# First feed-forward of a decoder layer: later activation sums, last differences used last, first half's residual by accumulating transfers, four squares later

## The chip, the cores and the metric

The kernel runs on one core of a Trainium2 chip. Its five engines work side by side, each through its own queue in order: TensorE (PE, matrix products), VectorE (DVE), ScalarE (ACT), GpSimd (POOL) and SyncE (SP, which here only starts transfers). An engine waits for another, or for a transfer, on semaphores. The metric is the device time of one execution in microseconds (us), lower is better; three runs of the kernel before took 2606.85, 2609.25 and 2610.62 us, so its median is 2609.25 us.

## The reference

One decoder layer on 1024 tokens of width 1024: a first SwiGLU feed-forward, a mixer (attention beside a state-space part), a cross-attention to a memory, and a second feed-forward. Each has a norm ahead and behind, and a residual. Only the first feed-forward and its residual matter here:

```python
def rmsnorm(x, g):
    return x * rsqrt(mean(x * x) + EPS) * g

def swiglu(h, w_gu, w_down):          # w_gu 1024 x 5632, w_down 2816 x 1024
    g, u = split(h @ w_gu, 2)
    return (silu(g) * u) @ w_down

h = x
f = swiglu(rmsnorm(h, ffn1_pre_g), ffn1_w_gu, ffn1_w_down)
h = h + 0.5 * rmsnorm(f, ffn1_post_g)
m = hybrid_mixer(rmsnorm(h, mix_pre_g), ...)      # goes on from h
```

## The kernel before

**Layout.** Activations lie transposed, features on the 128 partitions and tokens along the free axis. The 1024 tokens are two halves of 512 (`hh` 0 and 1), so one tile is 128x512. The 1024 model features are eight such tiles (`d` 0 to 7), the 2816 hidden features are 22 (`f` 0 to 21). A product in nearly full precision is made of three passes on TensorE: every operand is split into a high and a low part (`split`: ScalarE casts the high part, VectorE subtracts it from the whole for the low part), and the passes are high x high, low x high, high x low. A block of weights against four tiles of activations is therefore 12 matmuls of 128x128 by 128x512.

**Up-phase (`up_phase`).** For `f` 0 to 2 gate and up products are made plainly. From `f` = 3 (`first_seven`) on, `seven(f)` makes gate and up of one `f` for both token halves as a 2x2 product of blocks by seven products instead of eight. In order: `product(a,B22)`, `product(b,B21)`, `product(c,S[1])`, `product(m6,S[4])`, `product(a,B12)`, `product(c,S[5])`, `product(b,B11)`. The last three go on into banks `a`, `c` and `b`, which hold an earlier product. Bank `c` is the one to watch: `S[1]` is made in it, VectorE then reads it (`e = d + c`, line 823, where `d` is a difference that GpSimd makes of two copies, line 818), and only after this may `S[5]` be added to it. VectorE also reads `a` after B12 (line 833) and `b` after B11 (line 843), and the last step of an `f` is a multiplication on GpSimd (line 844).

The weight blocks of one `f` come from `pieces(f)`: seven sums and differences of quarters of the weights (GpSimd, line 757, tile `wc`), each then split into `whi`/`wlo`/`blk`. The fifth of them is a plain quarter (G0), the one that B12 takes, and is split from the loaded weights without a sum. The activations of B12 are tiles 0 to 3 of half 1: their low parts are the `xl` tiles numbered 28 to 31 below, made of differences (line 730) late in the run-up to `f` = 3.

**What sets the order.** Most side work is put into a list `later` with a due time on a model clock (`self.clock`) that advances with the matmuls written so far; when it is due it is written into the program there (`kp` keeps the place). Such work is: `act_sums`, which loads four stored activation tiles of two `f` back (line 609), makes five sums of them on VectorE (line 616) and stores these (line 621) for the down-phase; it runs for `f` 0 and 1 at `seven(4)` and for `f` 2 and 3 at `seven(5)`. `prepare_all`, which loads, splits and stores 62 half weight tiles for the mixer, one each 3.9 us of model time from 148 us on. What is written with `urgent` goes ahead of the queue of the scheduler.

**Down-phase (`down1`, `down7`).** Again seven products per pair of blocks, `m` = 0 to 6; weights `hl`, `wlo`, `whi`, `dx` are formed on VectorE (`cb`, line 1031) and split. As outputs become complete, `finish(m,i)` starts the norm behind: squares are summed (`squares`, `sumsq`: ScalarE squares, VectorE adds, line 363), `post` makes the factor rows, and per tile `apply(d)` multiplies (line 401), adds the residual that `resid` had loaded by a GpSimd transfer into `XL` (line 405), stores the new residual `h` by a GpSimd transfer (line 410), and casts the high part of the next input on ScalarE (`xh`, line 412). `low(d)` makes its low part (line 417) and `presum(d)` its square sums. Half 0 is finished while the products of `m` = 4 to 6 run, half 1 behind `m` = 6. Half 1's squares 0 to 3 are made during `m` = 6, its squares 4 to 7 as the last outputs come.

Of the kernel before, what the change touches and what calls it, by code (L numbers as in the profile page):

```python
# [14 lines left out]
ALU = mybir.AluOpType  # L15
# [32 lines left out]
class Kern:  # L48
# [189 lines left out]
    def prepare_all(self, sp):  # L238
        names = [("ssd", i) for i in [*range(6), *range(12, 26)]] + [("qkv", i) for i in range(QKV)]
        pairs = [  # L240
            ((self.fp, "acc0", None), (self.fp, "acc1", None)), ((self.fp, "rpost", None), (self.tp, "dg", None)),
            ((sp, "bh", None), (sp, "bl", None)),
        ]
        raw = [(sp, "braw", 2), (sp, "braw", 2), (self.xp, "xl0", KT + 1), (self.xp, "xl1", KT + 1)]
        n = 2 * len(names)
        self.prepare(names, raw, pairs, [148000 + 3900 * i for i in range(n)])

# [131 lines left out]

    def post(self, hh, gname, r2, gnext=None, out=None, step=None, spread=True, pins=(23000, 28000), accs=None, at=None, tail=None, hold=False):  # L380


        nc = self.nc
        t1, t2 = 2500, 6000
        if accs is None:
            accs = self.new_accs()
            for d in range(KT):
                self.sumsq(accs, d, self.F[hh][d])
# [9 lines left out]
        def apply(d):  # L398
# [4 lines left out]
                )  # L403
            )
            self.kp(nc.vector.tensor_tensor(out=F, in0=F, in1=self.XL[hh][d], op=ALU.add))  # L405
# [24 lines left out]

        def rest(d):
            low(d)
            presum(d)
# [16 lines left out]
        for d in range(KT):  # L450
            t = t3 + step * d
            q.append((t, lambda d=d: apply(d)))
            if out is None:
                q.append((t + min(step, 2600) + 300, lambda d=d: rest(d)))
        if out is None:
            t += min(step, 2600)
            c2 = self.t(self.rp, [P, 4], F32, f"cpre{hh}", bufs=2)
# [98 lines left out]
    def up_phase(self, sp, sp2, wgu, gpre, act_d, bank, load, plain, sizes, rw=None, begin=None):  # L556
# [40 lines left out]
        def act_sums(j, t0):  # L597

            x = {}
            names = ("a11", "a21", "a12", "a22")  # L600
            late = 14000 if begin else 9000

# [22 lines left out]
            for i, (n, out, a, b, op) in enumerate((  # L625
# [120 lines left out]
        def pieces(f):  # L746
# [3 lines left out]
            G0, G1, U0, U1 = G[:, 0:4], G[:, 4:8], U[:, 0:4], U[:, 4:8]  # L750
            for a, b, op in (
                (G0, G1, ALU.add), (U1, None, None), (G0, U1, ALU.add), (U0, G0, ALU.subtract), (G0, None, None),
                (G1, U1, ALU.subtract), (U0, U1, ALU.add),
            ):
                if b is not None:
                    t = self.t(sp if begin else sp2, [P, 4, P], F32, "wc", bufs=NWC)
                    inst = nc.gpsimd.tensor_tensor(out=t, in0=a, in1=b, op=op)  # L757
                    if begin and f == first_seven and a is G0 and b is G1:
                        self.tc.keep_in_program_order(inst)
# [44 lines left out]
        def seven(f):  # L804


            t5, d = (self.t(self.tp, [P, H], F32, f"sq{i}") for i in range(2))
            if later_sums and (f in (4, 5) if begin else f > 6 and f % 2):
                act_sums(later_sums.pop(0), self.clock)
# [19 lines left out]
            t1 = ft()  # L829
            with self.urgent():  # L830
                scaled(t1, a, 1)
            with self.urgent():
                nc.vector.tensor_tensor(out=e, in0=e, in1=a, op=ALU.add)
            product(c, S[5], True)
# [7 lines left out]
            with self.urgent():  # L842
                nc.vector.tensor_tensor(out=e, in0=e, in1=b, op=ALU.subtract)  # L843
            nc.gpsimd.tensor_tensor(out=t1, in0=t1, in1=e, op=ALU.mult)  # L844
            if f < 4:
# [106 lines left out]
    def down1(self, sp, wdn, act_d, xs_d, gpost, gnext):  # L952
# [7 lines left out]
        def squares(hh, d, tag):  # L960
            if d == 0:
                accs[:] = self.new_accs(tag)
            self.sumsq(accs, d, self.F[hh][d])

# [1431 lines left out]
```

## Time and profile before

| what | before |
|---|---|
| runs | 2606.85, 2609.25, 2610.62 us |
| profiled execution | span 2606.7 us from first to last instruction; no time outside the span is given for it |
| TensorE (PE) | 2578.2 us busy, 99% of the span, 12850 matmuls |
| VectorE (DVE) | 1993.9 us, 76% |
| ScalarE (ACT) | 1289.7 us, 49% |
| GpSimd (POOL) | 577.9 us, 22% |
| mean TensorE clock that was granted | 0.999 |

The profile is one execution, recorded by the hardware. A row of a timeline reads: start, duration (both in us), engine, source line, operation, output<-inputs by the program's names without buffer numbers, shapes, count; in square brackets how long the engine sat idle ahead of it and what released it. Several like instructions in a row are joined, with their count at the end. A PE row of 0.39 us is one matmul in a pipeline: its start and the next one's start matter, not its duration. In the windows view each stretch of time shows busy time and count of each engine, the granted clock (PEclk), the DMA share and the bytes moved.

Times of day in the span: `seven(3)` begins at about 79 us, `seven(4)` at about 102 us, the down-phase at about 449 us, half 0's norm is applied from 614 to 646 us, and the last down product ends at about 667 us.

### The profile page before, as it was taken

The numbers are of one execution on the slowest core, as the hardware profiler recorded it, in microseconds if no ns is written. First come the engines' busy times: TensorE is split into PE (matmuls) and PEld (weight loads), VectorE is DVE, ScalarE is ACT, GpSimd is POOL, SyncE is SP. The second block draws the span as 40 slices with busy tenths as digits, with TensorE's granted clock in tenths as the row PEclk, the third lists the DMA queues.
The fourth block names the chain that finished last, engine by engine and source line by source line (L and its number), as shares of the span: only waits on it lengthen the run. The fifth ranks groups of instructions, "written<-read, shape, count | busy, mean of one in ns | idle before, by whom it ended". The sixth has DMA issues, their size and how long they took to land.

```text
span 2606.7 us, 36814 instructions
## 1 busy us (share of the span) xinstructions
PE 2578.2 (99%) x12850; PEld 2148.5 (82%) x12850; DVE 1993.9 (76%) x3044; ACT 1289.7 (49%) x2300; POOL 577.9 (22%) x669
## 2 busy tenths in 40 slices
PE   9999999999999999999999999999999999999999
PEld 7788888888777778888888898888878888888887
DVE  7978987779689884777777777876656888777767
ACT  7434444555356663555555554445554433334543
POOL 2655554001000001111111110101011655551000
PEclk9999999999999999999999999999999999999999
DMA  6468887655656516555555556547558453326554
GB/s 241 158 210 298 300 287 272 209 188 169 224 195 204 182 69 213 162 149 152 141 152 131 169 161 215 206 153 250 196 185 299 146 183 104 109 85 236 184 174 154
DMA packets 216042, 489.82 MB, mean 188 GB/s; under 512 B 26544, under 2 KB 35120, under 8 KB 215856
## 3 DMA queue, kind: packets, MB, share of 16 engines
q1 hardware_dynamic: 169232, 381.02, 44.6%
q0 software_dynamic: 22720, 62.93, 8.1%
q10 hardware_dynamic: 23904, 43.53, 4.5%
q8 instruction: 101, 1.65, 0.3%
q14 instruction: 85, 0.70, 0.1%
HBM read 327.46 MB, written 138.94 MB: 179 GB/s over the span
## 4 chain that ended last, share of the span: by engine, by line
PE 77%; issue 13%; DVE 5%; ACT 1%; DMA 1%; POOL 0%; DVEq 0%; ACTq 0%; POOLq 0%
PE mm L139 38%; PE dn L139 34%; PE z L139 2%; PE tr L142 2%; PE ms L139 1%; PE ms L142 1%; DVE nb L1770 1%; DVE wlo L263 0%; DVE acc L363 0%; DVE hl L263 0%; DVE atl L263 0%; DVE F L1053 0%; DVE xl L263 0%; DVE F L405 0%; DVE xl L417 0%
## 5 line engine op out<-in xcount | busy, mean ns | idle before, releaser
L139 PE MATMUL mm<-xh,whi 128*128 128x512 f32 x1320 | 520.3, 403 | 2.5 <-ACT xh L268 1.1
L139 PE MATMUL mm<-xh,wlo 128*128 128x512 f32 x1272 | 488.7, 391 | 0.0
L139 PE MATMUL mm<-xl,whi 128*128 128x512 f32 (+1 forms) x1252 | 486.9, 389 | 1.8 <-DVE xl L263 1.4
L139 PEld LDWEIGHTS mm<-xh,whi 128*128 128x128 f32 x1320 | 248.2, 188 | 44.6 <-issue 3.8
L139 PEld LDWEIGHTS mm<-xh,wlo 128*128 128x128 f32 x1272 | 238.8, 188 | 52.1 <-DVE wlo L263 0.4
L139 PEld LDWEIGHTS mm<-xl,whi 128*128 128x128 f32 x1252 | 236.1, 189 | 35.9 <-DVE xl L263 2.3
L1770 DVE TENSOR_TENSOR_SCAN nb<-nb,begin 128x128 f32<-128x128 f32 (+7 forms) x128 | 171.3, 1351 | 50.8 <-ACT nb L1766 49.8
L1766 ACT ACTIVATE nb<-z,scale 128x128 f32<-128x128 f32 (+2 forms) x192 | 107.8, 581 | 78.8 <-PE z L139 78.6
L263 DVE TENSOR_TENSOR wlo<-wraw,whi 128x1024 fp32r<-128x1024 f32 x70 | 85.5, 1222 | 54.3 <-ACT whi L261 54.0
L261 ACT CAST whi<-wraw 128x1024 fp32r<-128x1024 f32 (+1 forms) x87 | 84.0, 965 | 78.3 <-PE mm L139 51.1
L658 ACT ACTIVATE ft<-ft 128x512 f32<-128x512 f32 x88 | 55.5, 631 | 99.3 <-DVE ft L657 97.3
L1787 POOL DMA_DIRECT2D mix<-sq x64 | 52.8, 826 | 231.0 <-DVE sq L1785 168.0
L139 PE MATMUL dn<-xh,wlo 128*128 128x512 f32 x296 | 101.3, 390 | 0.0
L757 POOL TENSOR_TENSOR wc<-raw,wraw 128x512 f32<-128x512 f32 x55 | 81.2, 1476 | 57.7 <-DVE blk L263 24.8
L263 DVE TENSOR_TENSOR atl<-tr,ath 128x512 fp32r<-128x512 f32 (+1 forms) x108 | 67.9, 632 | 31.2 <-ACT ath L261 30.8
L757 POOL TENSOR_TENSOR wc<-wraw,raw 128x512 f32<-128x512 f32 x56 | 80.2, 1432 | 50.9 <-DVE whi L263 16.6
L844 POOL TENSOR_TENSOR ft<-ft,e 128x512 f32<-128x512 f32 x37 | 59.7, 1614 | 121.2 <-DVE e L843 45.8
L139 PE MATMUL mm<-ath,v 128*128 128x256 f32 x320 | 85.9, 291 | 0.8 <-ACT sq L1784 0.6
L261 ACT CAST ath<-tr 128x512 fp32r<-128x512 f32 (+1 forms) x108 | 58.9, 546 | 53.3 <-PE tr L142 48.9
L139 PE MATMUL dn<-xh,blk 128*128 128x512 f32 x264 | 85.1, 389 | 0.0
L261 ACT CAST wlo<-wc 128x512 fp32r<-128x512 f32 x79 | 49.1, 621 | 69.9 <-PE dn L139 23.2
L139 PE MATMUL mm<-atl,v 128*128 128x256 f32 x320 | 82.8, 281 | 0.7 <-DVE atl L263 0.7
(579 smaller groups left out, 6775.6 us busy)
## 6 DMA issues: line engine op xcount, KB each, us to landing
whi<-dwhi SPq DMA_DIRECT2D x82, 512.0 KB, 3.6
wlo<-dwlo SPq DMA_DIRECT2D x82, 512.0 KB, 4.7
wraw<-in_w_gu SPq DMA_DIRECT2D x43, 512.0 KB, 4.0
dwhi<-bh SPq DMA_DIRECT2D x78, 256.0 KB, 4.1
dwlo<-bl SPq DMA_DIRECT2D x78, 256.0 KB, 3.9
raw<-in_w_gu SPq DMA_DIRECT2D x37, 512.0 KB, 4.0
wraw<-xs SPq DMA_DIRECT2D x56, 256.0 KB, 3.0
xs<-ft ACTq DMA_DIRECT2D x54, 256.0 KB, 3.7
```

The lines of the kernel that those rows point to most:

```text
L139: self._pe(self.nc.tensor.matmul(out, lhsT, rhs, start=start, stop=stop, skip_group_check=self.more), cost)
L142: self._pe(self.nc.tensor.transpose(out, src, self.ident if ident is None else ident), 109.0)
L261: self.kp(self.nc.scalar.copy(hi, src))
L263: self.nc.vector.tensor_tensor(out=lo, in0=src, in1=hi.bitcast(F32), op=ALU.subtract)
L658: nc.scalar.activation(t, t, AF.Silu)
L757: inst = nc.gpsimd.tensor_tensor(out=t, in0=a, in1=b, op=op)
L844: nc.gpsimd.tensor_tensor(out=t1, in0=t1, in1=e, op=ALU.mult)
L1766: nc.scalar.activation(nb[:, s0:s1], z[:, 0:n], AF.Sigmoid, scale=sc[:, i : i + 1])
L1770: nc.vector.tensor_tensor_scan(out=nb[:, 0:Wd][:, ::-1], data0=nb[:, 0:Wd][:, ::-1], data1=begin[:, S - Wd : S][:, ::-1], initial=0.0, op0 ...
L1787: nc.gpsimd.dma_start(out=self.mix_d[p][a * 64 : a * 64 + 64, csl], in_=o, accum_op=ALU.add)
```

## The change

Six places change, all of them in the first feed-forward but one (the product order, which the second feed-forward's first `seven` shares).

1. `prepare_all`: half weights from 170 us on, one each 3.8 us of model time.
2. `act_sums` of the first feed-forward runs at `seven(5)` and `seven(7)`; its sums come 9 us of model time after its start and its stores 4 us after the sums.
3. `seven(first_seven)`: `product(a,B12)` and the two VectorE steps behind it (now in `top()`) come last, behind B11. `pieces(first_seven)` gives the G0 block last to match. The first block's sum G0+G1 is made on VectorE, ahead of its place on GpSimd.
4. `post(fused=True)` for half 0: no residual is loaded to `XL` and VectorE doesn't add it. GpSimd starts a transfer per tile that adds the old residual in DRAM to `F` in SBUF (`accum_op=add`). Store, high part, low part and square sums of that tile (`settle`, `low`, `presum`) are due 10 us of model time behind the multiplication.
5. The factors of the next norm are due 9.5 and 13 us behind, not 17 and 20.5.
6. Half 1's squares 4 to 7 come first, as their outputs come; squares 0 to 3 follow behind `m` = 6.

```diff
-        self.prepare(names, raw, pairs, [148000 + 3900 * i for i in range(n)])
+        self.prepare(names, raw, pairs, [170000 + 3800 * i for i in range(n)])
...
+            if fused:
+                self.kp(nc.gpsimd.dma_start(out=F, in_=res[d], accum_op=ALU.add))
+                return
             self.kp(nc.vector.tensor_tensor(out=F, in0=F, in1=self.XL[hh][d], op=ALU.add))
...
+            settle(d)
+
+        def settle(d):
+            F = self.F[hh][d]
             self.XL[hh][d] = self.xl(hh, F32R)
             self.kp(nc.gpsimd.dma_start(out=self.h[hh][d], in_=F))
...
         def rest(d):
+            if fused:
+                settle(d)
             low(d)
             presum(d)
...
-                q.append((t + min(step, 2600) + 300, lambda d=d: rest(d)))
+                q.append((t + (10000 if fused else min(step, 2600) + 300), lambda d=d: rest(d)))
...
-            late = 14000 if begin else 9000
+            late = 9000
...
-                at(t0 + late + 3000 + 1200 * i, put, n)
+                at(t0 + late + (4000 if begin else 3000) + 1200 * i, put, n)
...
+            if f == first_seven:
+                parts.append(parts.pop(4))
...
-                    inst = nc.gpsimd.tensor_tensor(out=t, in0=a, in1=b, op=op)
+                    early = begin and f == first_seven and b is G1
+                    inst = (nc.vector if early else nc.gpsimd).tensor_tensor(out=t, in0=a, in1=b, op=op)
...
-            if later_sums and (f in (4, 5) if begin else f > 6 and f % 2):
+            if later_sums and (f in (5, 7) if begin else f > 6 and f % 2):
...
-            product(a, B12, True)
...
+            def top():
+                product(a, B12, True)
+                t1 = gated[1] = ft()
...
+            if f != first_seven:
+                top()
             product(c, S[5], True)
...
+            if f == first_seven:
+                top()
...
-                self.resid(0, 3500, 16000)
...
-                self.post(0, gpost, self.C[0], gnext, step=2600, accs=accs[:], tail=(17000, 20500))
+                self.post(0, gpost, self.C[0], gnext, step=2600, accs=accs[:], tail=(9500, 13000), fused=True)
             elif m == 5:
-                for d in range(4):
-                    at(17000 + 2500 * d, squares, 1, d, "bh")
...
             elif m == 6:
                 squares(1, 4 + i, "bh")
+                if i == 3:
+                    for d in range(4):
+                        at(500 + 1200 * d, squares, 1, d, "bh")
```

Three places show how instructions move. The rows are in the order of each engine's queue.

**VectorE in `seven(3)`.** `e_184` on its first line is the read of bank `c` (`dn_996` before, `dn_998` after), `xl_28` to `xl_31` are the low parts that B12 needs. Before, with the rows around that read:

```order
L730 SCALAR_TENSOR_TENSOR cb_892<-cb_892,params_78,cb_893 128x512
L263 TENSOR_TENSOR xl_28_104<-braw_815,xh_12_88 128x512
L823 TENSOR_TENSOR e_184<-sq_270_950,dn_996 128x512
L263 TENSOR_TENSOR wlo_974<-wc_972,wlo_974 128x512
L263 TENSOR_TENSOR xl_29_105<-rpost_835,xh_13_89 128x512
L263 TENSOR_TENSOR xl_30_106<-acc_259_873,xh_14_90 128x512
L827 TENSOR_TENSOR e_184<-e_184,dn_1017 128x512
L263 TENSOR_TENSOR blk_999<-wc_997,blk_999 128x512
L263 TENSOR_TENSOR xl_31_107<-cb_892,xh_15_91 128x512
```

And after the change:

```order
L740 SCALAR_TENSOR_TENSOR cb_892<-cb_892,params_78,cb_893 128x512
L263 TENSOR_TENSOR xl_28_104<-braw_815,xh_12_88 128x512
L263 TENSOR_TENSOR wlo_976<-wc_974,wlo_976 128x512
L837 TENSOR_TENSOR e_184<-sq_270_950,dn_998 128x512
L263 TENSOR_TENSOR xl_29_105<-rpost_835,xh_13_89 128x512
L263 TENSOR_TENSOR xl_30_106<-acc_259_873,xh_14_90 128x512
L263 TENSOR_TENSOR xl_31_107<-cb_892,xh_15_91 128x512
L263 TENSOR_TENSOR blk_1020<-wc_1018,blk_1020 128x512
L841 TENSOR_TENSOR e_184<-e_184,dn_1017 128x512
```

The differences are written in nearly the same places, while on TensorE the product that needs them comes two products later, and `S[5]`, which waits for the read of `dn`, comes one product earlier. A weight block (`wlo_976`) stands ahead of that read now.

**VectorE in `seven(4)`.** Here `e_1165` (before) and `e_1157` (after) are the read of bank `c`, and the rows of line 616 are the sums of `act_sums`. Before:

```order
L263 TENSOR_TENSOR blk_1192<-raw_283_1025,blk_1192 128x512
L263 TENSOR_TENSOR blk_1213<-wc_1211,blk_1213 128x512
L616 TENSOR_TENSOR xl_128_374<-cb_1107,cb_1112 128x512
L616 TENSOR_TENSOR xl_129_375<-cb_1109,cb_1107 128x512
L263 TENSOR_TENSOR blk_1236<-wc_1234,blk_1236 128x512
L616 TENSOR_TENSOR cb_1107<-cb_1107,dg_1115 128x512
L616 TENSOR_TENSOR cb_1112<-cb_1112,dg_1115 128x512
L823 TENSOR_TENSOR e_1165<-sq_292_1101,mm_1147 128x512
```

After:

```order
L667 TENSOR_TENSOR ft_1095<-mm_951,rpre_113_348 128x512
L850 TENSOR_TENSOR e_184<-e_184,mm_951 128x512
L263 TENSOR_TENSOR blk_1184<-raw_283_1025,blk_1184 128x512
L263 TENSOR_TENSOR blk_1205<-wc_1203,blk_1205 128x512
L263 TENSOR_TENSOR blk_1226<-wc_1224,blk_1226 128x512
L837 TENSOR_TENSOR e_1157<-sq_292_1101,mm_1139 128x512
```

Four sums are gone from ahead of the read; what B12 leaves of `seven(3)` (`mm_951`, the first two rows) has come in its place.

**ScalarE at the end of the down-phase.** `xh_1258` and `xh_1259` are the high parts of half 0's last two tiles (each waits, after the change, for its accumulating transfer), `wlo`, `dx` the last weights of the down-phase. Before:

```order
L412 ACTIVATE xh_1267_5769<-F_974_4356,params_78 128x512
L362 ACTIVATE sq_1350_6155<-F_973_4355 128x512
L362 ACTIVATE sq_1355_6182<-F_974_4356 128x512
L261 CAST wlo_6194<-cb_6192 128x512
L362 ACTIVATE sq_1372_6285<-ft_4342 128x512
L261 CAST dx_6217<-cb_6215 128x512
L261 CAST dx_6240<-cb_6238 128x512
```

After:

```order
L420 ACTIVATE xh_1258_5752<-F_973_4353,params_78 128x512
L362 ACTIVATE sq_1353_6201<-F_973_4353 128x512
L420 ACTIVATE xh_1259_5753<-F_974_4354,params_78 128x512
L261 CAST wlo_6157<-cb_6155 128x512
L362 ACTIVATE sq_1359_6231<-F_974_4354 128x512
L261 CAST dx_6187<-cb_6185 128x512
L261 CAST dx_6217<-cb_6215 128x512
```

The casts of the last weights stand behind the two high parts in both programs; what those wait for was VectorE's addition and is now a transfer. A square of half 1 has left the place between the casts.

More of the change, by code (lines that the diff above doesn't have):

```diff
@@ L378, in resid, with post @@
         self.later += [(self.clock + start + step * d, lambda d=d: one(d)) for d in range(KT)]
-    def post(self, hh, gname, r2, gnext=None, out=None, step=None, spread=True, pins=(23000, 28000), accs=None, at=None, tail=None, hold=False):
+    def post(self, hh, gname, r2, gnext=None, out=None, step=None, spread=True, pins=(23000, 28000), accs=None, at=None, tail=None, hold=False, fused=False):
         nc = self.nc
         t1, t2 = 2500, 6000
+        res = self.h[hh]
         if accs is None:
@@ L453, in post @@
             if out is None:
-                q.append((t + min(step, 2600) + 300, lambda d=d: rest(d)))
+                q.append((t + (10000 if fused else min(step, 2600) + 300), lambda d=d: rest(d)))
         if out is None:
-            t += min(step, 2600)
+            t += 10000 if fused else min(step, 2600)
             c2 = self.t(self.rp, [P, 4], F32, f"cpre{hh}", bufs=2)
@@ L750, in pieces @@
             G0, G1, U0, U1 = G[:, 0:4], G[:, 4:8], U[:, 0:4], U[:, 4:8]
-            for a, b, op in (
+            parts = [
                 (G0, G1, ALU.add), (U1, None, None), (G0, U1, ALU.add), (U0, G0, ALU.subtract), (G0, None, None),
                 (G1, U1, ALU.subtract), (U0, U1, ALU.add),
-            ):
+            ]
+            if f == first_seven:
+                parts.append(parts.pop(4))
+            for a, b, op in parts:
                 if b is not None:
                     t = self.t(sp if begin else sp2, [P, 4, P], F32, "wc", bufs=NWC)
-                    inst = nc.gpsimd.tensor_tensor(out=t, in0=a, in1=b, op=op)
-                    if begin and f == first_seven and a is G0 and b is G1:
+                    early = begin and f == first_seven and b is G1
+                    inst = (nc.vector if early else nc.gpsimd).tensor_tensor(out=t, in0=a, in1=b, op=op)
+                    if early:
                         self.tc.keep_in_program_order(inst)
@@ L827, in seven @@
                 nc.vector.tensor_tensor(out=e, in0=e, in1=m6, op=ALU.add)
-            product(a, B12, True)
[L829 to L833, printed above, removed]
+            gated = {}
+            def top():
+                product(a, B12, True)
+                t1 = gated[1] = ft()
+                with self.urgent():
+                    scaled(t1, a, 1)
+                with self.urgent():
+                    nc.vector.tensor_tensor(out=e, in0=e, in1=a, op=ALU.add)
+            if f != first_seven:
+                top()
             product(c, S[5], True)
@@ L843, in seven @@
                 nc.vector.tensor_tensor(out=e, in0=e, in1=b, op=ALU.subtract)
+            if f == first_seven:
+                top()
+            t1 = gated[1]
             nc.gpsimd.tensor_tensor(out=t1, in0=t1, in1=e, op=ALU.mult)
@@ L960, in squares @@
         def squares(hh, d, tag):
-            if d == 0:
+            first = (0, 4)[hh]
+            if d == first:
                 accs[:] = self.new_accs(tag)
-            self.sumsq(accs, d, self.F[hh][d])
+            self.sumsq(accs, d - first, self.F[hh][d])
         def at(t, f, *args):
```

## The prediction

> **What bounds the kernel now.** The first part of the page, the busy time of each engine, says that TensorE is nearly always at work:
>
> ```profile
> span 2606.7 us, 36814 instructions
> PE 2578.2 (99%) x12850; PEld 2148.5 (82%) x12850; DVE 1993.9 (76%) x3044; ACT 1289.7 (49%) x2300; POOL 577.9 (22%) x669
> ```
>
> The change takes no matmul away. It can only gain where TensorE stood still or ran slowly inside the first feed-forward, so I looked there next, in the windows view (per stretch: busy time and count of each engine, clock, DMA share, GB/s):
>
> ```profile
> 70.00:100.00 30.00, 27.62 (x119) 21.61 (x118) 28.38 (x32) 15.57 (x28) 16.47 (x16) 1.00 0.46 150
> 100.00:130.00 30.00, 27.00 (x113) 21.92 (x112) 27.04 (x31) 10.88 (x19) 21.64 (x15) 0.94 0.48 167
> 200.00:300.00 100.00, 100.00 (x442) 82.80 (x442) 89.31 (x116) 46.32 (x82) 59.72 (x38) 1.00 0.87 297
> 640.00:660.00 20.00, 18.30 (x74) 13.84 (x73) 17.53 (x30) 9.47 (x16) 5.33 (x10) 0.91 0.93 332
> ```
>
> At 200 to 300 us TensorE is full: 442 matmuls in 100 us, 0.226 us each. Three stretches are not, and two of them had a lower clock too (0.94 and 0.91). The waits view names who ended those gaps (total, times, longest):
>
> ```profile
> PE mm L139 <- DVE e L823: 3.8, 2, 3.0
> ...
> PE mm L139 <- DVE xl L263: 1.4, 2, 0.8
> ...
> PE mm L139 <- ACT whi L261: 0.9, 1, 0.9
> ...
> PE dn L139 <- DVE hl L263: 0.8, 1, 0.8
> ...
> PE dn L139 <- ACT dx L261: 0.5, 1, 0.5
> ...
> PE dn L139 <- DVE dx L263: 0.4, 1, 0.4
> ```
>
> And the timeline of TensorE gives each loss, start against start:
>
> ```profile
> 78.94 0.39 PE L139 MATMUL mm<-xh,wlo 128*128 128x512 f32 x1
> 80.27 0.50 PE L139 MATMUL mm<-xh,whi 128*128 128x512 f32 x1 [0.94 <-ACT whi L261]
> ...
> 92.69 0.61 PE L139 MATMUL mm<-xh,whi 128*128 128x512 f32 x2
> 93.90 0.50 PE L139 MATMUL mm<-xl,whi 128*128 128x512 f32 x1 [0.60 <-DVE xl L263]
> 94.23 0.63 PE L139 MATMUL mm<-xh,whi 128*128 128x512 f32 x2
> 95.70 0.50 PE L139 MATMUL mm<-xl,whi 128*128 128x512 f32 x1 [0.84 <-DVE xl L263]
> ...
> 115.10 0.39 PE L139 MATMUL dn<-xh,whi 128*128 128x512 f32 x1
> 118.48 4.41 PE L139 MATMUL mm<-S,wlo 128*128 128x512 f32 x12 [3.00 <-DVE e L823]
> 122.73 0.40 PE L139 MATMUL dn<-xh,whi 128*128 128x512 f32 x1
> ...
> 650.24 0.39 PE L139 MATMUL dn<-hl,wlo 128*128 128x512 f32 x1
> ...
> 657.80 0.40 PE L139 MATMUL dn<-hl,dx 128*128 128x512 f32 x1
> ```
>
> - `seven(3)`: 78.94 to 80.27 is 1.33 for one matmul, 1.1 lost. 92.69 to 95.70 is 3.01 for five matmuls (1.13), 1.9 lost. Together with a slow restart **3.3 us**, for the first weight block and for B12's differences (`xl`).
> - `seven(4)`: 115.10 to 118.48 loses 3.15, and the twelve matmuls behind it take 4.25 instead of 2.72, 1.5 more. **4.7 us**, for the read of bank `c`.
> - End of the down-phase: 15 matmuls between 650.24 and 657.80 take 7.56 instead of 3.40. **4.2 us**, for the last weights `hl` and `dx`.
>
> That is 12.2 us, all that the change can gain. Behind each place TensorE is full again, so a gain is carried to the end.
>
> **The product order and the first block (seven 3).** What made VectorE late:
>
> ```profile
> 71.25 2.21 DVE L263 TENSOR_TENSOR xl<-bh,xh 128x512 fp32r<-128x512 f32 x1
> ...
> 90.27 0.68 DVE L823 TENSOR_TENSOR e<-sq,dn 128x512 f32<-128x512 f32 x1
> ```
> ```profile
> 71.59 1.31 POOL L757 TENSOR_TENSOR wc<-wraw 128x512 f32<-128x512 f32 x1
> ...
> 86.98 1.55 POOL L818 TENSOR_TENSOR sq<-sq,sq 128x512 f32<-128x512 f32 x1 [0.82 <-ACT sq L817]
> ```
>
> A VectorE operation of 0.68 takes 2.21 beside GpSimd's sum of 1.31. With that sum on VectorE (0.68 more there, about 1.5 of blocking less) its cast no longer stands behind the gate's at 80 us: four rows earlier in its queue, some 3 us, against 1.1 late. That stall goes. B12 now starts two products (5.4 us) later, at 95.5 on a TensorE without stalls (working below), while its differences stand as before right behind the read of `c`: three rows of 0.60 behind 91, so they are all done by 93, 2 to 3 us early. These 3.3 us go.
>
> A new wait comes. Four products behind 79.17 (78.94 plus 0.23), at 79.17 + 4 x 2.72 = 90.05, `S[5]` wants bank `c`, and VectorE must have read it. Before, that read began at 90.27 and nobody cared. It can't start before GpSimd's difference (86.98 + 1.55, some 1.1 earlier in the new program). VectorE's queue ahead of it holds three rows more between the gate's product and it than before (3 x 0.60), less the 1.2 that it idled for the first block there: it ends at 91, give or take a half. **I take 1.0 us lost, bounds 0 and 2.0.** Net: 2.3 gained. The second feed-forward's first `seven` changes order too, but without differences in front of it on VectorE; cost nothing, up to 1 if the same wait shows.
>
> **The sums (seven 4, 5, 7).** The read of `c` in `seven(4)`:
>
> ```profile
> 113.28 1.73 POOL L818 TENSOR_TENSOR sq<-sq,sq 128x512 f32<-128x512 f32 x1
> ```
> ```profile
> 115.48 2.35 DVE L616 TENSOR_TENSOR cb<-cb,dg 128x512 f32<-128x512 f32 x2
> 117.75 0.68 DVE L823 TENSOR_TENSOR e<-sq,mm 128x512 f32<-128x512 f32 x1
> ...
> 134.41 1.29 DVE L616 TENSOR_TENSOR xl<-cb,cb 128x512 f32<-128x512 f32 x2 [4.13 <-DMA cb<-act]
> ```
>
> GpSimd's difference ended at 115.01; without the sums ahead the read would end by 115.7, against 115.33 (115.10 plus 0.23) wanted. So the sums owe 2.7 of the 3.15, and 0.4 would stay. Against that, B12's tail of `seven(3)` now reaches into `seven(4)`: VectorE's last two steps, GpSimd's multiplication (1.67) and a store that waits for it, all ahead of the two copies from which that difference is made. **I take 1.0 lost of the 4.7, so 3.7 gained; bounds 0 and 4.7.**
>
> One price hangs on the clock. Gaps of 0.60 and 0.84 within 2.4 us (92.9 to 95.7) left the clock at 1.00 in that stretch; 3.00 in one, and 1.7 in three within 3.5 us (650.5 to 653.8), were each followed by 3.4 us at half clock, for some 1.5 us. So a single wait of 1 us costs itself. The Trainium skill, "TensorE: Matmul & The Clock Gate", section "What's actually happening", has the clock halved after at least one idle window of about 3.4 us. By that, none of these gaps would have cost clock; the trace shows two that did, and it decides.
>
> At `seven(5)` the sums stood before, too: VectorE idled 4.13 us for their loads at 134.41 and TensorE did not wait. At 7 the engine has what the 200 to 300 row shows: 89% busy beside a full TensorE. Cost nothing by that cover, 0.7 per sum that is in the way. The half weights start 22 us later and so leave VectorE free for the sums; the last is due some 16 us later than before, at model 409, and all of this still lies in the stretch where TensorE is full. Cost nothing; if the down-phase found itself without buffers, a wait of about 1 us each.
>
> **The down-phase.** VectorE runs without a pause from 640 to the last `dx`:
>
> ```profile
> 645.02 0.77 DVE L401 SCALAR_TENSOR_TENSOR F<-F,params,rpost 128x512 f32<-128x512 f32 x1
> ...
> 646.28 0.71 DVE L405 TENSOR_TENSOR F<-F,xl 128x512 f32<-128x512 f32 x1
> ...
> 653.63 0.71 DVE L263 TENSOR_TENSOR hl<-raw,hl 128x512 fp32r<-128x512 f32 x1
> 654.23 0.71 DVE L263 TENSOR_TENSOR dx<-cb,dx 128x512 fp32r<-128x512 f32 x1
> ```
>
> Eight additions like that at 646.28, at a pitch of 0.60 (653.63 to 654.23), go: 4.8 us. The last `dx` would be ready at 650.1 instead of 654.9; TensorE unstalled would want it at about 651.4 (653.79 less the 2.4 lost until there). All of the 4.2 us would go. But ScalarE holds the last `xh`, and VectorE the last low part, ahead of the casts and the split of `dx`, and both now wait for a transfer instead of an addition. No row shows an accumulating transfer. The nearest:
>
> ```profile
> h<-F POOLq DMA_DIRECT2D x8, 256.0 KB, 2.3
> ...
> xl<-in_xT POOLq DMA_DIRECT2D x8, 256.0 KB, 10.2
> ```
>
> A store of the same 256 KB on GpSimd's queue in this stretch lands in 2.3 us, loads that are queued eight at a time in 10.2. ```profile
> 653.17 0.62 ACT L261 CAST dx<-cb 128x512 fp32r<-128x512 f32 x1 [0.58 <-DVE cb L1031]
> ```
>
> The last multiplication stands 18 rows (10.8 us) ahead of the last `dx` (649.4 now), at 638.6, and takes 0.77, its transfer's issue about 0.5. Behind the landing come five ScalarE steps (`xh`, `wlo`, a square, two `dx`) at 0.62 and a split of 0.71: 3.8. So landing may take 651.4 - 639.9 - 3.8 = 7.7 us, if VectorE runs 4.8 us ahead all the way. It hardly can, since loads of the weights wait for buffers that TensorE frees; I reckon with 5, and each us more costs one. The transfers start one by one like the store, but read DRAM and change SBUF: I expect about 5 to 7. **I take 2.5 gained; bounds 4.2 gained (landing in 2.3) and 2.5 lost (10.2, so 5.2 late, and the half clock stays: 4.2 - 1.5 - 5.2).**
>
> The Trainium skill, "SBUF — State Buffer", section "SBUF: two separate sides", warns that a transfer issued from GpSimd can be held up while VectorE keeps the port that writes its descriptors. By that, each accumulating transfer would be some 2.5 us late (its figures are 0.62 alone, 3.1 beside VectorE) and the forecast for this place would be about 0 gained. The store's 2.3 us with VectorE full is against it.
>
> Half 1's squares move behind `m` = 6:
>
> ```profile
> 669.92 0.30 ACT L261 CAST dtw<-dtraw 128x128 fp32r<-128x128 f32 x1 [1.80 <-DMA dtraw<-in_w_dt]
> ```
> ```profile
> 673.53 0.95 PE L139 MATMUL ms<-small,bh 128*128 128x1 f32 x8
> ```
>
> Their column sums start at 673.53, 4.2 earlier when the stalls are gone: 669.3. Four squares at 0.7 behind the last output (662.5) end by 667.5. Cost nothing; but that cast stands ahead of the last two squares, and if its load doesn't come earlier with TensorE, 2.9 is lost.
>
> **Sum.** 2.3 + 3.7 + 2.5 = 8.5 us. The profiled execution spans 2606.7, and gets 2598.2; its own time is not given apart, the three runs lie 0.2 to 4.0 above its span with the median 2.6 above. From the median: 2609.25 - 8.5 = 2600.8.
>
> **Rivals.**
> - All gaps close (no new wait on `c`, landing under 5 us): 12.2 gained, 2597.1. For it: the reads of `c` are late by little. Against: VectorE's queue is dense around 85 to 92.
> - The wait moves instead of going. `S[5]` waits 2.0 in `seven(3)`, and in `seven(4)` it waits 3 us again behind the tail of B12, half clock with it; 3.3 - 2.0 + 0 and 1 in the down-phase: 2.3 gained, 2607.0. For it: the chain VectorE, GpSimd, store, copies is new and in series. Against: GpSimd's difference was done at 115.01 even beside four sums' contention.
> - The accumulating transfers are slow, and the change is slower than before: if one takes two passes, each like a queued load, 20 us, it is 15 late, and the clock stays low: 4.2 - 1.5 - 15 = 12.3 lost here, 6.0 gained early, 2615.6. It decides from a landing of 13.7 us on (6.0 + 2.7 = 8.7 late, no gain in all); from 19 on it is over 0.2% slower. Against: 2.3 us of the plain store.
> - Early gains are there, but nothing at the down-phase (landing about 7.7): 2603.3, inside the forecast's own width.
>
> **How the numbers follow.** Forecast, with its bounds from 2598 to 2604: 0.57. All gaps close: 0.15. The wait moves: 0.17. Slow transfers: 0.06. None of it shows, for a cause that I don't see: 0.05. About 0.2% (5.2 us) is what a measurement of this kernel can tell from no change. Faster is the forecast and the first rival, 0.72; same 0.21; slower 0.07. The range takes in the first rival with a little for the runs' spread and reaches to the wait that moves: 2596 to 2607.
>
> **What would show it.** No gap at 79 and 92 to 96; a gap of about 1 before `S[5]` near 90, released by VectorE's `e`; at 115 a gap under 1.5 and PEclk 1.00; VectorE's idle time near the accumulating transfers; TensorE at 650 to 657 with 15 matmuls in under 5 us. The prediction is wrong if `e` is late by 2 or more in `seven(3)` or `seven(4)`, or if the landing exceeds 10.

## The result, and the profile after

The change makes the kernel slightly slower: 2611.93 us against 2609.25 us, medians of 21 runs each; the ratio is 1.0013 with a 95% interval of 1.0007 to 1.0019. The prediction, 2600.8 us in a range of 2596 to 2607, was wrong in sign.

The first part of the page after the change:

```profile
span 2610.8 us, 36791 instructions
PE 2581.3 (99%) x12850; PEld 2151.5 (82%) x12850; DVE 1982.2 (76%) x3037; ACT 1289.8 (49%) x2300; POOL 576.7 (22%) x668
```

VectorE is busy for 11.7 us less, so it was relieved as intended, and yet the span is 4.1 us longer. The windows view of the same stretches as before, and of two more (columns: busy time and count of PE, weight loads, DVE, ACT and POOL, clock, DMA share, GB/s):

```profile
70.00:100.00 30.00, 29.70 (x131) 24.29 (x130) 28.07 (x33) 15.25 (x28) 17.60 (x16) 1.00 0.42 139
100.00:130.00 30.00, 29.18 (x129) 23.85 (x128) 25.11 (x32) 11.87 (x21) 18.66 (x13) 1.00 0.49 176
600.00:640.00 40.00, 38.07 (x169) 31.29 (x168) 33.24 (x58) 21.24 (x36) 10.06 (x14) 0.96 0.78 210
640.00:660.00 20.00, 17.42 (x66) 13.01 (x65) 11.19 (x18) 4.90 (x9) 5.67 (x11) 0.83 0.94 341
2040.00:2060.00 20.00, 16.79 (x68) 13.48 (x67) 18.60 (x22) 10.68 (x19) 13.04 (x9) 0.91 0.31 113
```

Before, the third and the fifth of these stretches were full:

```profile
600.00:640.00 40.00, 40.00 (x186) 33.40 (x185) 38.88 (x67) 22.45 (x38) 3.24 (x6) 1.00 0.50 165
2040.00:2060.00 20.00, 19.91 (x89) 16.14 (x88) 19.92 (x25) 11.56 (x20) 13.14 (x9) 1.00 0.29 104
```

The first two rows gained what was meant to be gained: 131 and 129 matmuls in 30 us instead of 119 and 113, at full clock. The others lost. Note VectorE in the third and fourth row: it is busy for 33.2 and 11.2 us where it was for 38.9 and 17.5 before. The timeline of TensorE shows each place:

```profile
90.82 1.39 PE L139 MATMUL dn<-S,whi 128*128 128x512 f32 x5 [0.30 <-DVE e L837]
...
113.69 1.65 PE L139 MATMUL mm<-S,wlo 128*128 128x512 f32 x6 [0.82 <-DVE e L837]
...
626.40 0.94 PE L139 MATMUL dn<-hl,wlo 128*128 128x512 f32 x3 [1.93 <-DVE ft L1077]
...
649.48 0.73 PE L139 MATMUL dn<-hl,dx 128*128 128x512 f32 x2 [0.75 <-ACT dx L261]
650.70 0.50 PE L139 MATMUL dn<-hl,dx 128*128 128x512 f32 x1 [0.48 <-DVE dx L263]
652.55 2.01 PE L139 MATMUL dn<-hl,dx 128*128 128x512 f32 x3 [1.35 <-ACT dx L261]
...
2054.55 2.04 PE L139 MATMUL dn<-S,whi 128*128 128x512 f32 x4 [3.21 <-DVE e L837]
```

For a balance I took, from the trace, each matmul's start to the next one's start less 0.2267 us (the pitch of a full TensorE), summed over a stretch; starts less than 0.2 us apart, which belong to smaller products, are left out. This "loss" counts gaps and half clock (stretches in which the granted clock was 0.50) together; what smaller products leave in it is a constant part, so differences matter.

| loss in us | before | after | forecast of the difference | difference |
|---|---|---|---|---|
| 60 to 100 (`seven(3)`) | 3.5 | 0.6 | -2.3 | -2.9 |
| 100 to 200 (`seven(4)` and on) | 4.7 | 1.1 | -3.7 | -3.6 |
| 600 to 640 (half 0 applied) | 0.2 | 4.1 | 0 | +3.8 |
| 640 to 700 (end of the down-phase) | 4.8 | 6.9 | -2.5 | +2.2 |
| 2000 to 2100 (second feed-forward's first `seven`) | 0.4 | 5.0 | 0 | +4.6 |

The five differences add up to +4.1, by which the spans differ too.

### The profile page after: what moved, and what is told of

Same layout as the page of the kernel before. It is cut to its first block, busy times and chain, and to the rows that moved or that the text cites. A ratio compares the mean times of both kernels' runs of the same rounds, so it can differ in the third digit from the quotient of the medians.

```text
span 2610.8 us, 36791 instructions
## 1 busy us (share of the span) xinstructions
PE 2581.3 (99%) x12850; PEld 2151.5 (82%) x12850; DVE 1982.2 (76%) x3037; ACT 1289.8 (49%) x2300; POOL 576.7 (22%) x668
## 5 line engine op out<-in xcount | busy, mean ns | idle before, releaser
L139 PE MATMUL mm<-xh,whi 128*128 128x512 f32 x1304 | 514.9, 403 | 1.3 <-ACT xh L268 0.8
L139 PE MATMUL mm<-xh,wlo 128*128 128x512 f32 x1288 | 494.0, 391 | 0.0
L261 ACT CAST whi<-wc 128x512 fp32r<-128x512 f32 x82 | 50.8, 620 | 66.6 <-PE dn L139 27.9
```

The lines of the kernel that those rows point to most:

```text
L139: self._pe(self.nc.tensor.matmul(out, lhsT, rhs, start=start, stop=stop, skip_group_check=self.more), cost)
L261: self.kp(self.nc.scalar.copy(hi, src))
```

## The experiments

Each time is set against the kernel before, measured in the same session; the ratio has its 95% interval behind it. Losses are of one profiled execution each. They differ from one execution to the next: the kernel with tiles 1, 3 and 5 (below) was profiled twice and lost 3.0 and 5.0 us in 640 to 700 us. So a difference of some 2 us between two single profiles of that stretch shows little.

**The product order of the second feed-forward undone** (its blocks' order too):

```diff
-            if f == first_seven:
+            if begin and f == first_seven:
                 parts.append(parts.pop(4))
...
-            if f != first_seven:
+            if not (begin and f == first_seven):
                 top()
...
-            if f == first_seven:
+            if begin and f == first_seven:
                 top()
```

> The changed kernel, but the second feed-forward keeps the old order of products and blocks. Theory: the 3.21 us wait of S5 for VectorE's e at 2051 us, with the half clock behind it 4.6 us, comes from S5 standing one product closer to the read of bank c. It goes: about 2607.3 us against 2611.9, ratio to before 0.9993, no gap over 1 us between 2040 and 2060. Rival: VectorE is late there for a cause of its own (a blocked sum on GpSimd), and the wait stays with another product: 2611.9.

Measured: 2608.01 us, ratio 0.9998 (0.9989 to 1.0007); loss in 2000 to 2100 us 0.4. The wait is gone, and by the two ratios (1.0013 and 0.9998) some 3.9 us with it. The theory holds. The rows that explain it stood in the trace of before. VectorE, before:

```profile
2053.00 0.68 DVE L823 TENSOR_TENSOR e<-sq,dn 128x512 f32<-128x512 f32 x1
```

TensorE, before:

```profile
2050.75 0.39 PE L139 MATMUL mm<-xh,whi 128*128 128x512 f32 x1
...
2053.73 3.02 PE L139 MATMUL dn<-S,wlo 128*128 128x512 f32 x12
```

And VectorE after:

```profile
2048.52 1.78 DVE L740 SCALAR_TENSOR_TENSOR blk<-blk,params 128x512 f32<-128x512 f32 x1
2050.22 1.78 DVE L263 TENSOR_TENSOR blk<-wraw,blk 128x512 fp32r<-128x512 f32 x1
...
2053.73 0.67 DVE L837 TENSOR_TENSOR e<-sq,dn 128x512 f32<-128x512 f32 x1
```

Before, the read of bank `c` ended at 2053.68 and `S[5]` began at 2053.73: no slack at all behind B12, which had begun at 2050.75. With B12 taken away from in front of it, `S[5]` wants the bank one product, 2.7 us, earlier, while VectorE reads it at about the same time as ever.

**The residual added on VectorE again:**

```diff
+                self.resid(0, 3500, 16000)
...
-                self.post(0, gpost, self.C[0], gnext, step=2600, accs=accs[:], tail=(9500, 13000), fused=True)
+                self.post(0, gpost, self.C[0], gnext, step=2600, accs=accs[:], tail=(17000, 20500))
```

> The changed kernel, but half 0's residual is loaded and added on VectorE as before (old due times of the next norm's factors too). Theory: the gaps at 624 us and at 648 to 658 us come from the accumulating transfers. TensorE's loss in 600 to 700 us falls from 11.0 to about 5, as before the change: about 2606 us, ratio 0.9987. Rival: they come from what else moved there (half 1's squares, half weights later), and stay: 2611.9.

Measured: 2608.55 us, ratio 1.0001 (0.9992 to 1.0010), by the ratios some 3 us below the changed kernel. Loss in 600 to 640 us 0.2, in 640 to 700 us 3.6, together 3.9 where the changed kernel has 11.0. So some 7 us there are owed to the transfers. (The earlier due times of the next norm's factors, undone with them, are no rival: they count from a base that lies 7.4 us later with the transfers, so the factors were due 19.5 us behind the last multiplication, and now 19.6.) The time came down by only 3 us. This one profile lost 1.1 us more than the changed kernel's between 200 and 600 us and 1.6 more at 900 to 950 us; whether such losses account for the rest in the other executions is not shown.

**Both undone:**

> Both of the last two at once; what is left of the change is the later sums, the new product order in the first feed-forward, the first block on VectorE and the later squares. Theory: the three causes are apart, so the early gain of 6.5 us stands alone: about 2602 us, ratio 0.9973. Rival: the early gain is used up later whatever is done: 2607 or more.

Measured: 2603.89 us, ratio 0.9980 (0.9971 to 0.9989). The early gain stands alone: losses 0.6, 1.1, 0.2, 3.7 and 0.4 in the five stretches of the table. (The later half weights are left of the change, too.) These are 7.6 us less than before, but the span of this execution is only 3.8 shorter: 2.9 us more were lost in it around 1440 us, a place where most other profiles lost nothing and that of the later sums alone lost 3.0. Nor are the 1.1 us less in 640 to 700 us a gain of what is left of the change: the three gaps of before are still there (0.83, 0.68 and 0.60 us lost, before 0.92, 0.69 and 0.59), only the half clock behind them is missing.

**Plain transfers in place of the accumulating ones** (with the second feed-forward's old order):

```diff
-                self.kp(nc.gpsimd.dma_start(out=F, in_=res[d], accum_op=ALU.add))
+                self.kp(nc.gpsimd.dma_start(out=F, in_=res[d]))
```

> The first of these four, with each accumulating transfer replaced by a plain copy of the same 256 KB into the same tile (so half 0's feed-forward output is left out of the residual). Theory a: adding makes a transfer hold the transfer engines long; without it weights land in about 3 to 4.5 us, the gap at 624 goes and the last transfer lands in under 5: 2601 to 2604 us. Theory b: any 256 KB at this place does it: as the first of these, 2607.

Measured: 2604.28 us, ratio 0.9983 (0.9975 to 0.9992). In 600 to 640 us 0.2 is lost, where the same kernel with accumulating transfers loses 2.2: adding is what costs there, as theory a has it. In 640 to 700 us 7.6 is lost all the same (8.4 with adding): this loss is not owed to adding. There theory a missed: the last transfer lands after 7.4 us, not in under 5, and ScalarE waits for it as it does in the changed kernel:

```profile
642.45 0.73 ACT L420 ACTIVATE xh<-F,params 128x512 fp32r<-128x512 f32 x1 [3.72 <-DMA F<-in_xT]
```

The transfer queues between 608 and 624 us show why the first differ. The kernel with accumulating transfers (packets, MB, share of the 16 engines' time; then per issue KB and median us to landing):

```profile
q0 software_dynamic: 656, 1.31, 45.3%
q1 hardware_dynamic: 1085, 1.96, 36.2%
...
F<-in_xT POOLq DMA_DIRECT2D x4, 256.0 KB, 7.8
wraw<-in_w_dn SPq DMA_DIRECT2D x2, 256.0 KB, 5.4
wraw<-xs SPq DMA_DIRECT2D x2, 256.0 KB, 6.3
```

And with plain ones:

```profile
q1 hardware_dynamic: 1391, 2.52, 50.3%
q0 software_dynamic: 498, 1.68, 31.5%
...
F<-in_xT POOLq DMA_DIRECT2D x5, 256.0 KB, 4.0
wraw<-in_w_dn SPq DMA_DIRECT2D x3, 256.0 KB, 3.9
wraw<-xs SPq DMA_DIRECT2D x3, 256.0 KB, 4.2
```

GpSimd's queue (q0) takes 35% of the transfer engines' time in these 16 us per MB with adding (45.3 / 1.31) and 19% without (31.5 / 1.68). SyncE's queue (q1), which loads the weights, takes about the same per MB in both, 18% and 20%; and yet its loads land after 5.4 and 6.3 us instead of 3.9 and 4.2.

**Accumulating for tiles 0 to 5 only**, 6 and 7 added on VectorE (`fused` becomes a tuple of tiles, and `resid` loads the others):

```diff
-            if fused:
+            if fused and d in fused:
                 self.kp(nc.gpsimd.dma_start(out=F, in_=res[d], accum_op=ALU.add))
```

> As the run with the second feed-forward's old order, but only tiles 0 to 5 of half 0 take the accumulating transfer; tiles 6 and 7 are loaded ahead and added on VectorE as before. Theory: the loss at 645 to 660 us comes from the last transfer (issued together with three 512 KB loads for the next stage, landed after 7.9 us), for which ScalarE's high part waits ahead of the last weights' casts. It falls from about 8 to under 4 us; the gap at 624 stays (2 to 4): about 2604 us. Rival: VectorE is late by then from the weights' loads held up earlier: the loss stays at 7 to 8, 2608.

Measured: 2604.74 us, ratio 0.9985 (0.9976 to 0.9994); 1.8 lost in 600 to 640 us, 5.1 in 640 to 700 where it had been 8.4. The direction is the theory's, the size lies between the two. In the changed kernel ScalarE's wait for the last transfer is plain:

```profile
646.22 0.72 ACT L420 ACTIVATE xh<-F,params 128x512 fp32r<-128x512 f32 x1 [3.84 <-DMA F<-in_xT]
```

and VectorE stands behind it:

```profile
647.48 0.69 DVE L263 TENSOR_TENSOR wlo<-cb,wlo 128x512 fp32r<-128x512 f32 x1 [4.50 <-ACT wlo L261]
```

With the last two tiles added, this wait is gone, and yet VectorE reaches the last `dx` late, busy all the way from 632 to 649 us.

**Accumulating for tiles 1, 3 and 5 only:**

> As the run with the second feed-forward's old order, but only tiles 1, 3 and 5 take the accumulating transfer, the other five are added on VectorE. Theory: it is the bunch of four transfers within 5 us that holds the transfer engines; one at a time each 5 us costs nothing, and VectorE is spared three additions (1.8 us): no gap at 624, loss in 640 to 700 us between 2 and 3.6, about 2602.5 us, ratio 0.9977. Rival: each accumulating transfer delays the weights wherever it is: 2604.5 or more.

Measured: 2602.40 us, ratio 0.9979 (0.9970 to 0.9988), the lowest median of the series, not told apart from the run with both undone. In 600 to 640 us 0.2 is lost, as before the change, and 3.0 in 640 to 700. The three transfers were issued at 615.4, 620.4 and 632.1 us, and the loads beside them were not held up:

```profile
wraw<-in_w_dn SPq DMA_DIRECT2D x3, 256.0 KB, 3.8
wraw<-xs SPq DMA_DIRECT2D x3, 256.0 KB, 4.6
...
F<-in_xT POOLq DMA_DIRECT2D x2, 256.0 KB, 4.3
```

Transfers one at a time cost TensorE nothing there and spare VectorE three additions; that this gains time is not shown. Its first profile lost 4.3 us at 472 us.

**Accumulating for tiles 0, 1 and 2 only**, as many transfers but close together:

> As the run with tiles 1, 3 and 5, but tiles 0, 1 and 2 take the accumulating transfer: as many transfers, but within 3 us of each other. Theory: it is the bunch that delays the weights' loads: loads of weights issued in that time land after 6 us or more, and VectorE idles 2 us or more for them at 615 to 622; TensorE loses 1 to 2 us in 600 to 640. Rival: the number of transfers decides (three cost nothing, eight cost 2 to 4): loads land in under 5 us and TensorE loses nothing there.

Measured: 2608.08 us, ratio 1.0000 (0.9990 to 1.0009), 1.3 lost in 600 to 640 us, against 0.2. VectorE of this kernel:

```profile
614.91 0.75 DVE L402 SCALAR_TENSOR_TENSOR F<-F,params,rpost 128x512 f32<-128x512 f32 x1
619.06 0.69 DVE L1056 TENSOR_TENSOR cb<-xl,wraw 128x512 f32<-128x512 f32 x1 [3.40 <-DMA wraw<-in_w_dn]
```

In the trace four loads of weights issued from 612.6 to 615.4 us landed after 6.4 to 6.7 us. In the run with tiles 1, 3 and 5 the same three transfers, further apart, let such loads land after 3.0 to 4.7. With the same number of transfers, their bunching decides. The end of the down-phase also lost 7.1 here, though no accumulating transfer is near: the idle 3.4 us are not made up. So that late stretch has two causes: VectorE that is behind since 619 and, in the changed kernel, the last transfer.

**Only the later sums and half weights**, on the kernel before:

> The kernel before with only the later activation sums and later half weights. Theory: the 3.0 us gap of seven(4) is owed to the sums: the loss in 100 to 200 us falls from 4.7 to under 1, that of 60 to 100 us stays 3.5: about 2605.0 us. Rival: VectorE comes into seven(4) late anyway: 2 us or more are left there.

Measured: 2604.47 us, ratio 0.9986 (0.9977 to 0.9995). Loss in 60 to 100 us 2.7, in 100 to 200 us 0.2: the 3.0 us gap was owed to the sums. That 60 to 100 us did not stay at 3.5 is owed to the gap at 79 us, which is 0.16 in this profile instead of 0.94 although the first block is made as before. So a part of that gap belongs to the execution, and what the first block's sum on VectorE is worth by itself is not shown.

**Only the first feed-forward's order and first block**, on the kernel before:

> The kernel before with only the first feed-forward's new product and block order and the first block's sum on VectorE. Theory: the loss in 60 to 100 us falls from 3.5 to 0.6 and that of 100 to 200 us stays 4.7: about 2606 us. Rival: with the sums still there, B12's tail makes S5 of seven(4) later still, and the wait moves instead of going: over 6 us in 100 to 200 us, 2608 or more.

Measured: 2607.59 us, ratio 0.9997 (0.9988 to 1.0007). Loss in 60 to 100 us 0.6, in 100 to 200 us 6.1:

```profile
116.66 1.56 PE L139 MATMUL mm<-S,wlo 128*128 128x512 f32 x4 [4.20 <-DVE e L837]
```

The wait of `seven(4)` was 3.00 and is 4.20 with the sums still there. The rival holds in that stretch, and the time lies between the two: the order alone wins 2.9 and hands 1.4 on to the next `f`. With the sums moved too, it adds 1.2 to the 5.3 that these save alone (of 8.2 lost before 2.9 is left with the sums alone, 1.7 with both).

**Half 1's squares in the old order**, from the kernel with both undone, one execution:

> The run with both losses undone, but with half 1's squares in their old order (0 to 3 during the last products). Theory: the four squares on VectorE among the last weights cost what their 0.6 us each put in the way: the loss in 640 to 700 us rises from 3.65 to about the 4.8 of before. Rival: they stand where VectorE has time, and it stays 3.65.

Measured: one time of 2604.27 us; loss in 640 to 700 us 3.8, against 3.7. The theory's 1.1 us are not there. In one profile each, a cost below some 2 us can't be excluded.

**Half weights at their old times**, from the kernel with tiles 1, 3 and 5:

> As the run with tiles 1, 3 and 5, but with the half weights due from 148 us on each 3.9 us, as before the change. Theory: the gap of 2.4 us at 472.5 us in that run (ScalarE late at the start of the down-phase, with the half clock 4.3 us lost) is the price of ending the half weights 16 us later: it goes, and the time falls to about 2598.5 us, ratio 0.9963; the 1.1 us in 100 to 200 us may grow to 2. Rival: that gap varies from execution to execution and has nothing to do with them: 2602.4 as there.

Measured: 2603.90 us, ratio 0.9988 (0.9979 to 0.9997). Nothing is lost at 472 us, but 1.2 at 209 us and 2.0 instead of 1.1 in 100 to 200 us; no gain.

**The kernel with tiles 1, 3 and 5 a second time:**

> The run with tiles 1, 3 and 5 once more, for a second profile. If the gap at 472.5 us belongs to the program, it is there again, within half a microsecond of 2.4; if it belongs to the execution, it is gone or of another size.

Measured: 2605.26 us in one time. The first profile of that kernel had

```profile
475.36 1.90 PE L139 MATMUL dn<-hl,dx 128*128 128x512 f32 x5 [2.44 <-ACT F L1108]
```

and the second

```profile
474.09 3.28 PE L139 MATMUL dn<-hl,dx 128*128 128x512 f32 x13 [1.38 <-ACT F L1108]
```

So its size belongs to the execution. Losses between 200 and 600 us were under 0.2 in six of the fourteen profiles, the kernel before and the changed kernel among them, and 0.5 to 4.3 in the others. Whether the later half weights take away a margin that this place had stays open: of the three profiles with the old times none lost more than 0.5 at 470 to 480 us, of the eleven with the later times six did (0.9 to 4.3) and five did not.

## Why the prediction was wrong, by its own steps

- **What bounds the kernel; the three places.** Right. The early places gained 6.5 us, 6.0 were forecast, and the run with both losses undone keeps the gain.
- **First block, differences, read of bank `c` in `seven(3)`.** Right: the gaps at 79 and 92 to 96 are gone (the one at 79 is smaller in one profile that leaves the first block as it was, so its part is not shown apart), and `S[5]` waits 0.30 (0.46 start to start) where 1.0 was taken.
- **Sums out of `seven(4)`.** Right, in both terms: with the sums alone moved 0.2 is left (0.4 was worked out), and B12's tail costs 1.0 (1.0 was taken).
- **The second feed-forward's first `seven`: "cost nothing, up to 1 if the same wait shows".** This step failed, by 4.6 us. Its reason, "without differences in front of it on VectorE", is false: lines 740 and 263 make them there too. The same working that was done for `seven(3)` would have given it. The read ended at 2053.68 and the bank would be wanted at 2050.75, where B12 began: 2.9 us late (3.21 in the event), with half clock behind it. The place was full before the change and so didn't turn up among the gaps; I looked only where TensorE had waited.
- **The down-phase: "landing may take 7.7 us, I reckon with 5, and expect about 5 to 7".** The landing itself was fairly well guessed: the eight took 3.6 to 7.9 us, the last one the longest. What failed is the account of who pays. I counted the instructions that wait for these transfers, and not the transfers that share the transfer engines with them. "The transfers start one by one like the store" was wrong for the first four, issued within 5 us (609.8 to 614.8): the multiplications come as soon as the factor rows are there. The weights' loads beside them landed after 5.4 to 9.1 us instead of 2.7 to 4.6, VectorE idled for them, and the banks were read 1.93 us late at 624: 3.8 us that no term or rival had, since the sum took nothing for 600 to 640 us. VectorE's idle time there of 5.1 us (2.38 and 2.68) uses up the 4.8 us of the additions spared. These are the two rows in the changed kernel:

```profile
616.66 0.69 DVE L1055 TENSOR_TENSOR cb<-xl,wraw 128x512 f32<-128x512 f32 x1 [2.38 <-DMA wraw<-in_w_dn]
...
621.23 0.69 DVE L1055 TENSOR_TENSOR cb<-xl,raw 128x512 f32<-128x512 f32 x1 [2.68 <-DMA raw<-in_w_dn]
```

- **The end of the down-phase**, 2.5 gained in the forecast, lost 2.2, so this term missed by 4.7 us. The wait that was priced (ScalarE's high part, ahead of the casts, for a late landing) is there: the last transfer left at 638.3 beside three 512 KB loads for the next stage (639.3 to 641.9) and landed after 7.9. By the prediction's own rate (5 us are free, each more costs one) this would still have gained 1.3 of the 4.2. It is not adding that makes it late: with plain transfers the last one, issued at the same place, landed after 7.4. Together with VectorE's lag, and with 6.8 us at half clock instead of the 3.4 of before, it outweighs the gain. The runs part the two roughly: 3.7 us are lost in 640 to 700 us with neither (both undone), 5.1 with the late weights alone (tiles 6 and 7 added), 7.6 with the late landing and weights nearly on time (plain transfers), 8.4 with both (the second feed-forward's old order). So the late landing is the larger part, as far as single profiles that differ by 2 us from one execution to the next can say.
- **Half 1's squares, sums at 5 and 7.** Cost nothing, as forecast. For the half weights it holds in the changed kernel's profile; in others it stays open.
- **Chances.** Each rival was about a wait that the change touches directly. None was a place where slack was used to the last tenth, or other traffic's delay. The signs of being wrong had the same blind spot: `e` was late by 0.5 and 1.0 in `seven(3)` and `seven(4)` and no accumulating transfer of the changed kernel took more than 7.9 us to land, so none of them showed.

The kernel with both losses undone (2603.89 us) and that with three spaced accumulating transfers (2602.40 us) are both faster than the kernel before by 0.2%.

## What to carry to other kernels

When a consumer is moved forward, look up its producer's end against the consumer's start at every place where the same code runs, also where nothing waits today: a row that ends 0.05 us ahead of its reader is a wait as soon as the reader moves. When a computation is handed to a transfer, the price is not only its landing but what it does to the loads beside it: spread such transfers out, and keep them away from bursts of other loads. An engine relieved of work gains nothing if the loads that feed it come later by as much.

## What the hardware showed that was not expected

An accumulating transfer from DRAM into SBUF held the transfer engines about 1.8 times as long per byte as a plain one in the same stretch (35% against 19% of 16 us per MB, the stores of that queue among it). One at a time it lands in 3.6 to 4.9 us, in a bunch the ones behind the first take 7 to 8. Being issued from GpSimd beside a full VectorE is not what makes it late, which the prediction had as a possibility after the Trainium skill, "SBUF — State Buffer", section "SBUF: two separate sides": the single ones are early with VectorE just as full (38.1 of 40 us in 600 to 640 us). That section speaks of VectorE operations in a 2-port mode, such as a copy; the rows here are operations on two inputs, so the prediction took it further than it goes.

A short wait costs clock from some point on, and where it falls matters as much as how long it is. In the fourteen profiles half clock came in stretches of 3.41 us or twice that (but for the last one, at the end of the program), and within one profile they start on one grid of 3.41 us: at 118.08 and 653.97 us in the kernel before, which is 157 times 3.413. I added up the lost time, as defined above, in every period of that grid (60 to 668 and 2000 to 2100 us, periods at full clock). Each of the 14 periods with 2.18 us or more was followed by half clock, and none of the others, with 2.07 at most. The grid lies differently against the program in each execution (its first line falls 0.6 to 3.4 us behind the first instruction), so the same gaps cost clock in one and not in another. At 624 us the changed kernel lost 2.19 us in one period:

```profile
624.29:627.70 3.41, 1.48 (x7) 1.12 (x7) 3.41 (x7) 2.99 (x6) 1.42 (x2) 1.00 0.68 189
627.70:631.11 3.41, 3.41 (x10) 2.67 (x9) 3.41 (x7) 0.00 (x0) 0.00 (x0) 0.50 0.90 273
```

The run with the second feed-forward's old order lost 1.95 there, and kept its clock (columns as above; the clock is the third number from the end):

```profile
623.44:626.85 3.41, 1.72 (x8) 1.15 (x7) 3.41 (x6) 3.19 (x6) 1.42 (x2) 1.00 0.65 175
626.85:630.26 3.41, 3.41 (x17) 2.79 (x16) 3.41 (x7) 0.21 (x1) 0.00 (x0) 1.00 0.99 283
```

Half clock is also most of what the 3.0 and 5.0 us of the kernel with tiles 1, 3 and 5 differ by: its gaps at the end of the down-phase fell into two periods in the first execution (1.5 at most) and into one in the second (2.25, with half clock behind). The Trainium skill, "TensorE: Matmul & The Clock Gate", section "What's actually happening", asks for an idle window of about 3.4 us; here less was enough, some 2.2 of 3.41.
